# A two-layer hybrid encoder in one launch: softmax ahead in the engines' order, later transposes, another spread of the convolution's taps

## The chip, the cores and the metric

The kernel runs on one core of a Trainium2 chip. The metric is the device time of one launch in microseconds (us). The kernel before takes 1797.9 us, the median of three runs (1797.21 to 1798.3).

Five engines of the core matter. TensorE (PE in the profile) multiplies matrices, VectorE (DVE) and ScalarE (ACT) work on elements and rows, GpSimd (POOL) does little here, and SyncE (SP) starts most DMAs. Each engine takes its own instructions strictly in order. Between engines there are semaphores.

## The reference

The input is a sequence of 512 rows of 1024 numbers, in float32. Two layers follow each other, and each of them computes:

```python
h = rmsnorm(x, norm_mix[i]);  proj = h @ w_in[i]
qa, ka, va, glu_in, qc, kc, vc, gates = split(proj)
ya = diff_attention(qa, ka, va, ...)          # 4 heads, two softmaxes each: a0 - lam * a1
yb = silu(layernorm(depthwise_conv31(a * sigmoid(g))))     # glu_in = a, g; 512 channels, 31 taps
yc = neighbourhood_attention(qc, kc, vc, rpb) # 8 heads, 8x16 window on an 8x64 grid
ga, gb, gc = split(sigmoid(gates))
x = x + (ga*(ya@w_br_a) + gb*(yb@w_br_b) + gc*(yc@w_br_c)) @ w_o[i]
x = x + (silu(rmsnorm(x)@w_ffn_gate) * (rmsnorm(x)@w_ffn_up)) @ w_ffn_down
x = x + sigmoid(rmsnorm(x)@w_ple_gate) * (p[i]@w_ple_in)
```

Here `lam = exp(sum(lq1*lk1)) - exp(sum(lq2*lk2)) + lam_init`, one number per layer, and a last RMSNorm ends the program.

## The kernel before

**Data and products.** Activations are kept transposed, as tiles of 128 channels by 512 rows. Every float32 operand is split into a high part and a low rest, both of type fp32r: ACT rounds the high part (`wh`, line 143) and DVE subtracts it (`wl`, line 157). One product is then three matmuls (`mm3`, lines 177 to 179). Weights come in blocks of up to 128x1024 through rings of three buffers named `wr` (raw), `wh` and `wl`. All blocks go through the same rings, the 256-wide ones of the embedding too (`pin_wh`). So the block three places later writes the buffer of the block that PE has read.

**Order of PE.** PE's order is fixed by the order of the code. A long projection calls `tick()` after every four chunks, that is after 12 matmuls. At each tick the pieces of attention whose time has come put their own matmuls in between. A piece is a generator, and `yield n` hands back until n ticks later.

**Order of the other engines.** A scheduler sets it beforehand, by priorities: mostly the order of the code. Weights get 400 places of lead. Nothing is reordered while the program runs, so an instruction whose input is late holds all behind it on its engine.

**The background taps.** The 124 tap operations of a layer's convolution (`conv_z`, line 160 and a first one at line 525, all on DVE) have slack. The function `background` ties so many of them behind a given instruction. The table `BG` says how many, by stage. They must all be done before the sums of the convolution's layer norm (`conv_ss`, then its split `conv_qk`, then PE's `conv_tr` at line 556).

**The neighbourhood units** (tiles `natten_...`, 16 a layer, `natten_unit`). Each unit issues two blocks of scores (`natten_sc`). DVE adds the bias and takes the minimum (`natten_b`, line 684), ACT exponentiates (`natten_e`), DVE inverts the sums (line 696) and ACT scales. After `yield 2` PE transposes the weights into `natten_tr` (five transposes, lines 708 to 712). ACT and DVE split these into `natten_pt` and the edge tile `natten_a`. After another `yield 2` PE multiplies by the values (`natten_av`, lines 730 and 731). The results go into `natten_y` through DVE.

**The differential units** (tiles `diff_...`). They have scores (`diff_sc`, line 798), a maximum on DVE (`diff_s`, line 895), two exponentials on ACT (`diff_a`, `diff_e`), a combination on DVE (`diff_a`, line 160), eight transposes (`diff_tr`, line 852) and products with the values (`diff_av`). The root-mean-square of a head goes through `diff_tr` as well (line 213, reduced on DVE at line 215 into `diff_sm`). The `diff_tr` tiles share a ring of two banks. The rotary embedding of the queries and keys is a row of DVE operations on `diff_rp`.

**The values** (`values()`, lines 591 to 593 in the profile) accumulate four blocks of the sequence in PSUM, the first three in three banks, the fourth in the bank of `natten_av`.

**Order of the stages in a layer:** gated linear unit, neighbourhood queries and keys and values, gates in between, differential queries and keys and values, `branchc`, `mergea`, one block of `gateb`, the convolution's norm, `mergeb`, output product, feed-forward, embedding.

Of the kernel before, what the change touches and what calls it, by code (L numbers as in the profile page):

```python
# [61 lines left out]
class Net:  # L62
# [246 lines left out]
    def opening(self):  # L309
# [22 lines left out]
        for k in range(KD):  # L332
# [7 lines left out]
            self.split(his[k], los[k], raws[k])  # L340
# [48 lines left out]
    def lambdas(self):  # L389
# [4 lines left out]
        self.tt(pr, lv[:, 0, :].rearrange("p (a b) -> p a b", b=64),  # L394
                lv[:, 1, :].rearrange("p (a b) -> p a b", b=64), ALU.mult)
# [6 lines left out]
        for i in range(L):  # L402
            v = self.nlam[:, i:i + 1]
            nc.vector.tensor_scalar(v, v, lam_init(i), -1.0, ALU.add, ALU.mult)
            nc.vector.tensor_scalar(self.subg[:, i:i + 1], self.par(i, "sub"),
                                    1.0 - lam_init(i), None, ALU.mult)

    def layer(self, i, h, xsrc, xs):
# [4 lines left out]
        if i == 0:  # L413
            self.lambdas()
# [5 lines left out]
        self.drain(self.renorm)  # L420
        self.h = self.hs
# [4 lines left out]
        self.gates(acc, gb, "cc")  # L426
        self.natten_in(3, sn, yc)
        self.gates(acc, gb, "c")
        self.diff_in(0, sd, ya)
        self.gates(acc, gb, "c")  # L430
# [3 lines left out]
        self.gates(acc, gb, "bb")  # L434
        self.diff_in(3, sd, ya)
        self.gates(acc, gb, "ccbbcc")
# [93 lines left out]
    def background(self, after, n):  # L530

        ph, self.phase = self.phase, "conv"
        for _ in range(n):
            i = next(self.todo, None)
            if i is not None:
                self.tc.add_manual_dep(
                    i.ins, after.ins.name,
                    mybir.DependencyInfo(mybir.DependencyClass.NoSync, mybir.DependencyReason.DATA),
                    reason="background")
        self.phase = ph  # L540

# [37 lines left out]
    def values(self, ap, parts):  # L579
# [33 lines left out]
    def natten_in(self, pr, st, ys):  # L613
# [5 lines left out]
        for s, off in enumerate((OFF_QC, OFF_KC)):  # L619
# [3 lines left out]
            if pr == 0:  # L623
# [5 lines left out]
            self.background(self.stt(low, ps, f, nat.bitcast(F32), ALU.mult, ALU.subtract),  # L629
                            self.bg["natten"] if pr or self.i else 0)  # L630
# [37 lines left out]
    def natten_unit(self, pr, half, u, st4, k2, st, box, y):  # L668
# [10 lines left out]
        for t in range(2):  # L679
# [4 lines left out]
            nc.vector.tensor_tensor_reduce(  # L684
                out=b[:, t], in0=sc, in1=b[:, t], scale=-1.0, scalar=3.0e38,
                op0=ALU.add, op1=ALU.min, accum_out=m[:, t:t + 1])
            wide = half != t
            e = two[:, t, 0:NW + 64 * wide]
            own = slice(64 * (qt == 1), 64 * (qt == 1) + NW)
            if wide:  # L690
                pad = slice(0, 64) if qt == 1 else slice(NW, NW + 64)
                nc.gpsimd.memset(e[:, pad], 0.0)
            self.act(e[:, own], b[:, t], AF.Exp, table="exp", scale=-1.0, bias=m[:, t:t + 1],
                     accum_out=m[:, 2 + t:3 + t])
# [44 lines left out]
    def gates(self, acc, gb, names):  # L739
        for n in names:  # L740
            if n == "c":
                self.gate_c(acc, next(self.ms[0]))
            else:
                self.gate_b(gb, next(self.ms[1]), AF.Copy, None)

    def gate_c(self, acc, m):
# [781 lines left out]
```

## Time and profile before

| What | Value |
|---|---|
| median of three runs | 1797.9 us |
| profiled execution, its own time | 1798.02 us |
| its span | 1796.2 us |
| time outside the span | 1.8 us |
| PE busy | 1773.8 us (99%) |
| DVE busy | 1372.2 us (76%) |
| ACT busy | 897.9 us (50%) |

The span is the time from the first to the last recorded instruction of the profiled execution. A busy share is a mean over stages. In the list of waits a row gives the waiting engine, its operation and line, the instruction that it waited for, and then the total, the number and the longest of these waits. A timeline row gives start, duration, engine, line, operation, output and inputs, and in brackets the idle time ahead of it. When several instructions are put into one row the duration is that of all of them. The window view gives, for a stretch of time, each engine's busy time and number of instructions, and then the clock that PE was granted (1.00 is full).

### The profile page before, as it was taken

The numbers are of one execution on the slowest core, as the hardware profiler recorded it, in microseconds if no ns is written. First come the engines' busy times: TensorE is split into PE (matmuls) and PEld (weight loads), VectorE is DVE, ScalarE is ACT, GpSimd is POOL, SyncE is SP. The second block draws the span as 40 slices with busy tenths as digits, with TensorE's granted clock in tenths as the row PEclk, the third lists the DMA queues.
The fourth block names the chain that finished last, engine by engine and source line by source line (L and its number), as shares of the span: only waits on it lengthen the run. The fifth ranks groups of instructions, "written<-read, shape, count | busy, mean of one in ns | idle before, by whom it ended". The sixth has DMA issues, their size and how long they took to land.

```text
span 1796.2 us, 26565 instructions
## 1 busy us (share of the span) xinstructions
PE 1773.8 (99%) x10020; PEld 1553.7 (86%) x10020; DVE 1372.2 (76%) x2112; ACT 897.9 (50%) x1481; POOL 63.5 (4%) x102
## 2 busy tenths in 40 slices
PE   9999999999999999999999999999999999999998
PEld 7887788888899899898878878888888998998987
DVE  7678789898887567587786777988878775775776
ACT  5556554525565245255545564563255552542544
POOL 0000000000000000000000000000000100000000
PEclk9999999999999999999999999999999999999999
DMA  5666444224656456253437664533354662663432
GB/s 186 186 183 171 126 126 106 88 88 159 211 145 182 145 146 191 91 138 121 158 113 194 174 159 127 137 85 99 107 186 152 184 195 73 188 180 110 119 109 95
DMA packets 98385, 257.51 MB, mean 143 GB/s; under 512 B 12881, under 2 KB 17617, under 8 KB 98257
## 3 DMA queue, kind: packets, MB, share of 16 engines
q1 hardware_dynamic: 90912, 231.00, 42.3%
q0 software_dynamic: 6336, 23.07, 7.1%
q8 instruction: 79, 1.29, 0.3%
q10 hardware_dynamic: 1008, 1.75, 0.3%
q14 instruction: 50, 0.40, 0.1%
HBM read 216.44 MB, written 7.86 MB: 125 GB/s over the span
## 4 chain that ended last, share of the span: by engine, by line
PE 93%; DVE 4%; ACT 1%; issue 1%; DMA 0%; POOL 0%; POOLq 0%; DVEq 0%; ACTq 0%
PE ffn_sc L1090 14%; PE ffn_av L1090 7%; PE ffn_mm L178 4%; PE ffn_mm L177 4%; PE ffn_mm L179 4%; PE ffn_tr L1090 4%; PE mergea_mm L177 2%; PE mergea_mm L178 2%; PE mergea_mm L179 2%; PE gatec_mm L178 2%; PE gatec_mm L179 2%; PE gatec_mm L177 2%; PE wo_mm L177 2%; PE wo_mm L178 2%; PE wo_mm L179 2%; PE diff_sc L798 2%
## 5 line engine op out<-in xcount | busy, mean ns | idle before, releaser
L143 ACT ACTIVATE ffn_wh<-ffn_wr 128x1024 fp32r<-128x1024 f32 (+1 forms) x114 | 117.3, 1029 | 183.2 <-PE ffn_mm L178 106.5
L160 DVE SCALAR_TENSOR_TENSOR conv_z<-glu_z,pre_par,conv_z 128x512 f32<-128x512 f32 x240 | 179.3, 747 | 2.9
L157 DVE TENSOR_TENSOR ffn_wl<-ffn_wr,ffn_wh 128x1024 fp32r<-128x1024 f32 (+1 forms) x114 | 134.9, 1184 | 42.5 <-ACT ffn_wh L143 42.0
L1090 PE MATMUL ffn_sc<-wo_h,ffn_wh 128*128 128x256 f32 x704 | 130.4, 283 | 0.0
L1090 PEld LDWEIGHTS ffn_sc<-wo_h,ffn_wh 128*128 128x128 f32 x704 | 110.4, 192 | 0.8
L1090 PE MATMUL ffn_sc<-wo_h,ffn_wl 128*128 128x256 f32 x352 | 99.6, 283 | 0.0
L177 PE MATMUL ffn_mm<-ffn_z,ffn_wh 128*128 128x512 f32 x240 | 93.5, 389 | 0.0
L178 PE MATMUL ffn_mm<-ffn_z,ffn_wh 128*128 128x512 f32 x240 | 93.4, 389 | 0.0
L179 PE MATMUL ffn_mm<-ffn_z,ffn_wl 128*128 128x512 f32 x240 | 93.4, 389 | 0.0
L157 DVE TENSOR_TENSOR ffn_t<-ffn_mm,wo_r 128x512 f32<-128x512 f32 x48 | 33.0, 688 | 76.2 <-PE ffn_mm L179 76.1
L157 DVE TENSOR_TENSOR ffn_wl<-ffn_rp,ffn_wh 128x1024 fp32r<-128x1024 f32 x44 | 53.7, 1221 | 30.0 <-ACT ffn_wh L143 30.0
L143 ACT ACTIVATE mergea_wh<-mergea_wr 128x1024 fp32r<-128x1024 f32 (+1 forms) x32 | 27.1, 847 | 88.8 <-PE mergea_mm L178 80.4
L1090 PEld LDWEIGHTS ffn_sc<-wo_h,ffn_wl 128*128 128x128 f32 x352 | 67.5, 192 | 0.0
L1090 PE MATMUL ffn_sc<-wo_qk,ffn_wh 128*128 128x256 f32 x352 | 67.2, 283 | 0.0
L1090 PE MATMUL ffn_sc<-wo_v,ffn_wh 128*128 128x256 f32 x352 | 67.1, 283 | 0.0
L1090 PE MATMUL ffn_av<-wo_h,ffn_wh 128*128 128x256 f32 x352 | 65.3, 283 | 0.0
L143 ACT ACTIVATE ffn_wh<-ffn_rp 128x1024 fp32r<-128x1024 f32 x44 | 46.4, 1055 | 29.3 <-PE ffn_mm L178 17.5
L143 ACT ACTIVATE natten_e<-natten_b,natten_s 128x256 f32<-128x256 f32 x64 | 32.2, 503 | 47.0 <-issue 42.8
L1090 PEld LDWEIGHTS ffn_sc<-wo_qk,ffn_wh 128*128 128x128 f32 x352 | 54.9, 192 | 0.0
L1090 PEld LDWEIGHTS ffn_av<-wo_h,ffn_wh 128*128 128x128 f32 x352 | 54.9, 192 | 0.0
L1090 PEld LDWEIGHTS ffn_sc<-wo_v,ffn_wh 128*128 128x128 f32 x352 | 54.9, 192 | 0.0
L179 PEld LDWEIGHTS ffn_mm<-ffn_z,ffn_wl 128*128 128x128 f32 x240 | 45.1, 188 | 9.4
(725 smaller groups left out, 5654.4 us busy)
## 6 DMA issues: line engine op xcount, KB each, us to landing
ffn_wr<-w_gu SPq DMA_DIRECT2D x66, 512.0 KB, 4.3
ffn_e<-w_gu SPq DMA_DIRECT2D x32, 512.0 KB, 3.7
ffn_e<-w_gu POOLq DMA_DIRECT2D x32, 512.0 KB, 7.8
ffn_wr<-w_fd SPq DMA_DIRECT2D x32, 512.0 KB, 4.5
natten_wr<-w_in SPq DMA_DIRECT2D x16, 512.0 KB, 4.4
natten_b<-bias SPq DMA_DIRECT2D x32, 256.0 KB, 3.4
gatec_wr<-w_in SPq DMA_DIRECT2D x16, 512.0 KB, 4.6
diff_wr<-w_in SPq DMA_DIRECT2D x16, 512.0 KB, 4.4
```

The lines of the kernel that those rows point to most:

```text
L143: i = self.nc.scalar.activation(out, in_, func, **kw)
L157: return self.nc.vector.tensor_tensor(out, a, b, op)
L160: return self.nc.vector.scalar_tensor_tensor(out, a, s, b, op0, op1)
L177: mm(out, wh, ah, start=first, stop=False)
L178: mm(out, wh, al, start=False, stop=False)
L179: mm(out, wl, ah, start=False, stop=last)
L798: self.nc.tensor.matmul(out, st4[:, u, qs], st[:, ks], start=n == 0, stop=n == 1)
L1090: mm(bank[:, u], w[:, u, kp], t, start=begin and n == 0, stop=False, skip_group_check=True)
```

## The change

It has seven parts.

1. The softmax operations on DVE and ACT, of the neighbourhood and the differential units, get 60 places of priority (`URGENT`).
2. A neighbourhood unit's transposes come three ticks after its scores rather than two.
3. The table of taps changes: two rather than one behind each differential operation that has them, numbers of their own for the gates, one more behind every second `branchc`.
4. `values()` goes through the product's chunks in three stretches (0 to 3, 4 and 5, 6 and 7). The fourth accumulator is taken later.
5. The computation of `lam` moves behind the first neighbourhood queries and keys, tied to `low`, an operation there.
6. The warm-up matmuls at the start are 9, not 10, and the first block's high part is rounded on DVE.
7. `behind()` is a helper that ties one instruction behind another.

Line numbers shift: 143 becomes 144, 157 becomes 158, 160 becomes 161, 177 to 179 become 178 to 180, 215 becomes 216, 895 becomes 910, 556 becomes 565.

```diff
-WARM = 10
-BG = dict(glu=2, natten=3, diff=1, gatec=2, branchc=1, gateb=5, mergea=4, mergea2=3)
+WARM = 9
+BG = dict(glu=2, natten=3, diff=2, branchc=1, mergea=4, mergea2=3)
+URGENT = 60
...
+            if k == 0:
+                nc.vector.tensor_copy(his[0], raws[0])
...
-        if i == 0:
-            self.lambdas()
...
         self.drain(self.renorm)
+        if i == 0:
+            self.lambdas()
...
-        self.gates(acc, gb, "cc")
+        self.gates(acc, gb, "cc", 2)
...
-        self.gates(acc, gb, "bb")
+        self.gates(acc, gb, "bb", 3)
...
-        self.gates(acc, gb, "ccbbcc")
+        self.gates(acc, gb, "ccbbcc", 1)
...
-        for t in range(3):
-            products(t, range(2))
-        for t in range(3):
-            products(t, range(2, 4))
+        for ks in (range(2), range(2, 4)):
+            for t in range(3):
+                products(t, ks)
+        for t in range(2):
+            products(t, range(4, 6))
         accs.append(self.ps("av"))
         products(3, range(4))
         vs = []
+        for t in range(2, 4):
+            products(t, range(4, 6))
         for t in range(4):
-            products(t, range(4, KD))
+            products(t, range(6, KD))
...
-            nc.vector.tensor_tensor_reduce(
+            with self.tc.high_priority(offset=URGENT):
+                nc.vector.tensor_tensor_reduce(
...
-        nc.vector.reciprocal(m[:, 4:6], m[:, 2:4])
-        for t, (_, own) in enumerate(es):
-            self.act(own, own, AF.Copy, scale=m[:, 4 + t:5 + t])
-        yield 2
+        with self.tc.high_priority(offset=URGENT):
+            nc.vector.reciprocal(m[:, 4:6], m[:, 2:4])
+            for t, (_, own) in enumerate(es):
+                self.act(own, own, AF.Copy, scale=m[:, 4 + t:5 + t])
+        yield 3
...
-            self.background(self.tt(acc[m], acc[m], ps, ALU.mult), self.bg["branchc"])
+            self.background(self.tt(acc[m], acc[m], ps, ALU.mult), self.bg["branchc"] + m % 2)
...
+            with self.tc.high_priority(offset=URGENT):
+                nc.vector.tensor_reduce(out=m[:, u:u + 1], in_=sc, op=ALU.max, axis=AX.X,
+                                        negate=True)
```

How the instructions stand is shown at three places of layer 0. The number behind a name tells one tile of that name from another.

**Place 1: DVE, between the last two neighbourhood units and the first differential unit.** `natten_tr_1977` and `natten_tr_1978` before, and `natten_tr_2041` and `natten_tr_2042` after, are the transposes of the sixteenth unit. Before:

```order
L157 TENSOR_TENSOR natten_y_1514<-natten_av_1968,natten_y_1514 64x256
L157 TENSOR_TENSOR natten_pt_1985<-natten_tr_1977,natten_pt_1985 128x512
L157 TENSOR_TENSOR natten_y_1514<-natten_y_1514,natten_av_1968 64x256
L157 TENSOR_TENSOR diff_rp_1921<-diff_rp_1921,diff_r_1589 128x512
L160 SCALAR_TENSOR_TENSOR conv_z_830<-glu_z_316,pre_par_67,conv_z_830 128x512
```

And now, from the second of the differential unit's reductions on; ahead of these rows stand, from the same `natten_y` on, `natten_y`, `natten_a_2043`, three operations on `diff_rp`, two taps and the unit's first reduction:

```order
L910 TENSOR_REDUCE diff_s_2066<-diff_sc_2073 128x1
L158 TENSOR_TENSOR diff_rp_1901<-diff_rp_1901,diff_kh_1829 128x512
L158 TENSOR_TENSOR diff_rp_1971<-diff_rp_1971,diff_r_1567 128x512
L917 RECIPROCAL diff_s_2066<-diff_s_2066 128x1
L161 SCALAR_TENSOR_TENSOR conv_z_1909<-glu_z_318,pre_par_67,conv_z_1909 128x512
L161 SCALAR_TENSOR_TENSOR diff_s_2066<-diff_s_2066,natten_nlam_540,diff_sm_1753 128x1
L161 SCALAR_TENSOR_TENSOR conv_z_1909<-glu_z_318,pre_par_67,conv_z_1909 128x512
L161 SCALAR_TENSOR_TENSOR diff_a_2071<-diff_e_2077,diff_s_2066,diff_a_2071 128x512
L158 TENSOR_TENSOR diff_rp_1971<-diff_rp_1971,diff_r_1569 128x512
L158 TENSOR_TENSOR natten_y_1491<-natten_y_1491,natten_av_2032 64x256
L158 TENSOR_TENSOR diff_rp_1971<-diff_rp_1971 128x512
L158 TENSOR_TENSOR natten_pt_2049<-natten_tr_2041,natten_pt_2049 128x512
```

`natten_pt` of the last unit moved from right behind the first `natten_y` to behind the whole softmax of the first differential unit. On PE the transposes of that unit are now followed by 12 matmuls of `values()`, the four score matmuls, 12 more of `values()`, and then `natten_av`, which reads `natten_pt_2049`.

**Place 2: DVE, in the differential units, from the second score reduction of one unit (the head's fourth) on to the reduction of `diff_tr` at line 215, or 216 now.** Before, the rows are 11:

```order
L895 TENSOR_REDUCE diff_s_2361<-diff_sc_2368 128x1
L157 TENSOR_TENSOR diff_rp_2298<-diff_rp_2298 128x512
L900 RECIPROCAL diff_s_2361<-diff_s_2361 128x1
L160 SCALAR_TENSOR_TENSOR diff_s_2361<-diff_s_2361,glu_nlam_435,diff_sm_2010 128x1
L160 SCALAR_TENSOR_TENSOR diff_a_2366<-diff_e_2372,diff_s_2361,diff_a_2366 128x512
L157 TENSOR_TENSOR diff_rp_2298<-diff_rp_2298,diff_kh_2237 128x512
L157 TENSOR_TENSOR diff_rp_2377<-diff_rp_2377,diff_r_1589 128x512
L525 TENSOR_SCALAR conv_z_2384<-glu_z_319,pre_par_67 128x512
L157 TENSOR_TENSOR diff_wl_2643<-diff_wr_2641,diff_wh_2642 128x1024
L157 TENSOR_TENSOR diff_rp_2377<-diff_rp_2377,diff_r_1591 128x512
L215 TENSOR_REDUCE diff_sm_2453<-diff_tr_2448 128x4
```

Now they are 19, of which these are the last 12:

```order
L161 SCALAR_TENSOR_TENSOR diff_a_2371<-diff_e_2377,diff_s_2366,diff_a_2371 128x512
L158 TENSOR_TENSOR diff_rp_2302<-diff_rp_2302 128x512
L158 TENSOR_TENSOR diff_rp_2302<-diff_rp_2302,diff_kh_2241 128x512
L158 TENSOR_TENSOR diff_rp_2382<-diff_rp_2382,diff_r_1567 128x512
L158 TENSOR_TENSOR diff_wl_2645<-diff_wr_2643,diff_wh_2644 128x1024
L161 SCALAR_TENSOR_TENSOR conv_z_1909<-glu_z_318,pre_par_67,conv_z_1909 128x512
L158 TENSOR_TENSOR diff_rp_2382<-diff_rp_2382,diff_r_1569 128x512
L161 SCALAR_TENSOR_TENSOR conv_z_1909<-glu_z_318,pre_par_67,conv_z_1909 128x512
L910 TENSOR_REDUCE diff_s_2464<-diff_sc_2465 128x1
L158 TENSOR_TENSOR diff_rp_2382<-diff_rp_2382 128x512
L910 TENSOR_REDUCE diff_s_2464<-diff_sc_2471 128x1
L216 TENSOR_REDUCE diff_sm_2458<-diff_tr_2453 128x4
```

From the first reduction of the unit, two rows ahead of these 19 and five ahead of the 11, to the reduction of `diff_tr`, there are now four taps rather than two, seven operations on `diff_rp` rather than six, and the next unit's two score reductions besides.

**Place 3: ACT and DVE at the convolution's norm.** `gateb_mm_3928` (before) and `gateb_mm_3927` (after) are the products that PE computes right ahead of `conv_tr`. ACT before:

```order
L143 ACTIVATE pin_e_3925<-pin_t_3923 128x512
L143 ACTIVATE conv_qk_3915<-conv_ss_3911 128x512
L143 ACTIVATE gateb_wh_4013<-gateb_wr_4012 128x1024
L143 ACTIVATE gateb_v_3977<-gateb_mm_3928 128x512
```

and now:

```order
L144 ACTIVATE pin_e_3924<-pin_t_3922 128x512
L144 ACTIVATE gateb_wh_4012<-gateb_wr_4011 128x1024
L144 ACTIVATE gateb_v_3976<-gateb_mm_3927 128x512
L144 ACTIVATE conv_qk_3914<-conv_ss_3910 128x512
```

DVE before:

```order
L157 TENSOR_TENSOR pin_e_3920<-pin_t_3918,pin_e_3920 128x512
L157 TENSOR_TENSOR gatec_x_3107<-gatec_x_3107,mergea_t_3883 128x512
L160 SCALAR_TENSOR_TENSOR conv_z_3642<-glu_z_924,pre_par_67,conv_z_3642 128x512
L157 TENSOR_TENSOR pin_e_3925<-pin_t_3923,pin_e_3925 128x512
L157 TENSOR_TENSOR conv_ss_3911<-conv_ss_3911,conv_z_3642 128x512
L157 TENSOR_TENSOR conv_qk_3915<-conv_ss_3911,conv_qk_3915 128x512
L157 TENSOR_TENSOR gateb_wl_4014<-gateb_wr_4012,gateb_wh_4013 128x1024
```

and now:

```order
L158 TENSOR_TENSOR gatec_x_3100<-gatec_x_3100,mergea_t_3878 128x512
L161 SCALAR_TENSOR_TENSOR conv_z_3662<-glu_z_902,pre_par_67,conv_z_3662 128x512
L158 TENSOR_TENSOR pin_e_3924<-pin_t_3922,pin_e_3924 128x512
L161 SCALAR_TENSOR_TENSOR conv_z_3662<-glu_z_902,pre_par_67,conv_z_3662 128x512 x3
L158 TENSOR_TENSOR gateb_wl_4013<-gateb_wr_4011,gateb_wh_4012 128x1024
L161 SCALAR_TENSOR_TENSOR conv_z_3662<-glu_z_902,pre_par_67,conv_z_3662 128x512
L158 TENSOR_TENSOR conv_ss_3910<-conv_ss_3910,conv_z_3662 128x512
L158 TENSOR_TENSOR conv_qk_3914<-conv_ss_3910,conv_qk_3914 128x512
```

Four more taps stand ahead of the last `conv_ss`, and the next weight block's split (`gateb_wh`, `gateb_wl`) moved from behind `conv_qk` to ahead of `conv_ss` and `conv_qk`. That block is the third in the ring behind the one that PE reads for the `gateb` product (two 256-wide `pin` blocks lie between), so it takes the same buffer.

More of the change, by code (lines that the diff above doesn't have):

```diff
@@ L535, in background, with behind @@
             if i is not None:
[L536 to L539, printed above, removed]
+                self.behind(i, after)
         self.phase = ph
+    def behind(self, i, after):
+        self.tc.add_manual_dep(
+            i.ins, after.ins.name,
+            mybir.DependencyInfo(mybir.DependencyClass.NoSync, mybir.DependencyReason.DATA),
+            reason="background")
     def conv(self, cs, ys):
@@ L737, in natten_unit, with gates, gate_c @@
         self.tt(y[rs, 1, qs], y[rs, 1, qs].bitcast(F32), av[ro], ALU.add)
[L739 to L742, printed above, removed]
-            else:
-                self.gate_b(gb, next(self.ms[1]), AF.Copy, None)
-    def gate_c(self, acc, m):
+    def gates(self, acc, gb, names, n):
+        for name in names:
+            if name == "c":
+                self.gate_c(acc, next(self.ms[0]), n)
+            else:
+                self.gate_b(gb, next(self.ms[1]), AF.Copy, None, n)
+    def gate_c(self, acc, m, n):
         self.phase = "gatec"
@@ L769, in merge_a, with gate_b @@
             self.background(self.tt(acc[m], acc[m], g, ALU.add), self.bg["mergea2"])
-    def gate_b(self, gs, m, func, table):
+    def gate_b(self, gs, m, func, table, n=5):
         self.phase = "gateb"
@@ L778, in gate_b @@
                 gs += self.parts_of("rp" if m == 2 else "v", [512], 2)
-        self.background(self.act(gs[m], ps, func, table=table), self.bg["gateb"])
+        self.background(self.act(gs[m], ps, func, table=table), n)
     def merge_b(self, ys, acc, gs):
```

58 lines of the change are left out of this document (30 added, 28 removed).

## The prediction

> **What bounds the kernel now.** First the page of the whole execution: busy shares, then the chain that ended last.
>
> ```profile
> PE 1773.8 (99%) x10020; PEld 1553.7 (86%) x10020; DVE 1372.2 (76%) x2112; ACT 897.9 (50%) x1481; POOL 63.5 (4%) x102
> PE 93%; DVE 4%; ACT 1%; issue 1%; DMA 0%; POOL 0%; POOLq 0%; DVEq 0%; ACTq 0%
> ```
>
> PE bounds it: 1796.2 − 1773.8 = 22.4 us of the span are left without PE. The change removes one warm-up matmul and no other work of PE. So the time can only move by PE's waits, and by the clock at which PE runs. Next, therefore, PE's waits:
>
> ```profile
> PE natten_tr L710 <- ACT natten_e L143: 5.1, 2, 2.5
> PE diff_sc L798 <- ACT diff_a L143: 2.3, 2, 1.2
> PE natten_mm L591 <- DVE natten_t L160: 1.7, 1, 1.7
> PE natten_tr L708 <- ACT natten_e L143: 1.6, 2, 0.8
> PE diff_av L591 <- DVE natten_y L157: 1.5, 2, 0.7
> PE diff_av L177 <- DVE diff_v L157: 0.9, 2, 0.5
> PE conv_tr L556 <- DVE conv_qk L157: 0.2, 1, 0.2
> PE conv_tr L556 <- ACT conv_qk L143: 0.2, 1, 0.2
> ```
>
> Those that come twice come once per layer. Then the windows around the longest of them (PE, PEld, DVE, ACT and POOL busy, then the clock):
>
> ```profile
> 174.31:177.72 3.41, 1.61 (x11) 1.36 (x12) 3.20 (x7) 2.77 (x8) 0.15 (x1) 1.00 0.77 193
> 177.73:181.14 3.41, 3.41 (x10) 2.63 (x9) 3.32 (x10) 1.63 (x5) 0.00 (x0) 0.50 0.33 123
> 54.84:58.25 3.41, 2.43 (x11) 2.02 (x12) 2.96 (x5) 1.32 (x2) 0.00 (x0) 1.00 0.94 231
> 1065.19:1068.60 3.41, 3.41 (x13) 2.94 (x14) 3.17 (x5) 1.17 (x3) 0.15 (x1) 0.50 0.72 223
> 352.00:413.50 61.50, 61.50 (x273) 50.96 (x272) 60.18 (x87) 16.44 (x24) 0.00 (x0) 1.00 0.34 104
> ```
>
> After each wait of 2.5 us stands a window of 3.41 us in which PE never stops but has a clock of 0.50. Half of that, **1.7 us**, is lost besides. The wait of 1.7 us at 54 us has no such window behind it. The last row says that DVE is busy 60.18 of 61.50 us ahead of the convolution's norm: there is no room there for work that comes late.
>
> **The waits that go.** Neighbourhood transposes come 12 matmuls later, and the softmax has priority. From the rows of waits, per layer: natten_tr 5.1/2 + 1.6/2 = 3.35, the half-clock window 1.7, diff_sc 2.3/2 = 1.15, diff_av 1.5/2 + 0.9/2 = 1.2. That is 7.4, and **14.8 us** for two layers. The bounds are nothing and this: a row cannot give more than it holds.
>
> At 52 us the wait for natten_t is 1.7. The work on lam that moves away was some small operations on DVE ahead of that chain and a table load on ACT (first row; the second is what PE waits for):
>
> ```profile
> 48.10 1.28 ACT L143 ACT_TABLE_LOAD   x1
> 52.02 0.68 DVE L160 SCALAR_TENSOR_TENSOR natten_t<-natten_t,natten_kh 128x512 fp32r<-128x512 f32 x1
> 5.88 0.80 PE L347 MATMUL pre_mm<-glu_v,pre_y 128*128 128x512 f32 x1 [0.19 <-ACT pre_y L143]
> ```
>
> I take 1.2 of the 1.7, between nothing and all. The third row is the first real matmul, which waited for ACT's rounding; DVE may have that sooner, for 0.3, between nothing and 0.6 (its rounding stood behind one other ACT operation). The gain is 14.8 + 1.5 = **16.3 us**.
>
> **The wait that comes at the last neighbourhood unit.** natten_pt of that unit now stands on DVE behind the first differential unit's softmax. Prices of the rows, from the timeline before at that place:
>
> ```profile
> 193.11 0.29 PE L708 MATMUL natten_tr<-pre_ident,natten_e 128*128 128x128 f32 x1
> 193.24 0.60 PE L710 MATMUL natten_tr<-pre_ident,natten_e 128*128 128x128 f32 x4
> 195.12 0.67 DVE L157 TENSOR_TENSOR natten_pt<-natten_tr,natten_pt 128x512 fp32r<-128x512 f32 x1
> 199.13 0.64 PE L730 MATMUL natten_av<-natten_pt,natten_v 128*128 128x256 f32 x4
> 199.96 0.40 PE L798 MATMUL diff_sc<-diff_x,diff_qk 128*128 128x512 f32 x1
> 202.36 0.75 DVE L160 SCALAR_TENSOR_TENSOR conv_z<-glu_z,pre_par,conv_z 128x512 f32<-128x512 f32 x1
> 203.74 0.42 DVE L157 TENSOR_TENSOR natten_y<-natten_y,natten_av 64x256 fp32r<-64x256 f32 x1
> 204.19 0.69 DVE L157 TENSOR_TENSOR diff_rp<-diff_rp 128x512 f32<-128x512 f32 x1
> 204.80 0.68 DVE L895 TENSOR_REDUCE diff_s<-diff_sc 128x1 f32<-128x512 f32 x1
> 206.38 0.16 DVE L900 RECIPROCAL diff_s<-diff_s 128x1 f32<-128x1 f32 x1
> 206.58 0.22 DVE L160 SCALAR_TENSOR_TENSOR diff_s<-diff_s,glu_nlam,diff_sm 128x1 f32<-128x1 f32 x1
> 206.84 0.75 DVE L160 SCALAR_TENSOR_TENSOR diff_a<-diff_e,diff_s,diff_a 128x512 f32<-128x512 f32 x1
> ```
>
> From start to start, an operation of 128x512 takes 0.61 (204.19 to 204.80), a tap 0.66 and diff_a 0.67 (about 0.08 less than its bar), natten_y 0.45 (203.74 to 204.19), the reciprocal 0.2, the small product 0.26. natten_pt took 0.67. Count from the end of the natten_av ahead of the last transposes. PE needs 0.5 for them, 24 matmuls at 0.227 (24 matmuls lie in the 5.4 us between 193.7 and 199.13), 5.45, and four score matmuls at the same price, 0.9: it wants natten_pt at **6.9**. DVE starts natten_y some 0.25 later and does natten_y 0.45, natten_a, which is half as wide, 0.3, three diff_rp 1.8 and two taps 1.2: 4.0. The scores are there by 3.9 (0.5 + 12 × 0.227 + 0.5 + 0.2). Then two reductions 1.2, four diff_rp 2.4, the reciprocal 0.2, two taps 1.3, small product 0.26, diff_a 0.67, natten_y 0.45, natten_pt 0.67: 4.0 + 7.2 = **11.2**. The wait is 11.2 − 6.9 = 4.3. It is longer than 2.5, so the half clock follows: 1.7. Two layers: **12.0 us**. Bounds per layer: 3 to 8, since the first eight rows may run while PE still multiplies, or DVE may arrive late by the 1.2 that natten_pt needed at 195.12 after its transposes.
>
> **The wait that comes in the differential units.** More taps and the next unit's reductions stand ahead of the diff_sm reduction, which frees one of the two diff_tr banks.
>
> ```profile
> 237.12 0.69 DVE L895 TENSOR_REDUCE diff_s<-diff_sc 128x1 f32<-128x512 f32 x1 [1.51 <-PE diff_sc L798]
> 247.08 0.68 DVE L215 TENSOR_REDUCE diff_sm<-diff_tr 128x4 f32<-128x512 f32 x1
> 248.39 1.04 PE L852 MATMUL diff_tr<-pre_ident,diff_a 128*128 128x128 f32 x8
> 252.03 0.60 PE L226 MATMUL diff_tr<-pre_ident,diff_rc 128*128 128x128 f32 x4
> ```
>
> At 237.12 DVE had waited for PE, so both orders start level there. To the end of diff_sm (247.7) the new order adds two taps, two reductions and one diff_rp, 3.1, less 0.5 that DVE stood idle for ACT: 250.3. PE needs the bank for the second four of its eight transposes, 248.8: a wait of 1.5. Then the transposes of 252.03 need the other bank, which DVE's split of the first four (diff_pt) frees: ahead of its end stand three taps, one diff_rp, diff_a, three small operations and diff_pt itself, 4.4 us. That ends at 254.7, against 252.03 + 1.5 when PE is there: another 1.2. Together 2.7 per layer, **5.4 us**, with no half clock, as behind the 1.7 at 54 us. Bounds per layer: nothing (DVE ahead by 3) and 2.7 + 1.7.
>
> **The wait that comes at the convolution of layer 0.**
>
> ```profile
> 409.04 0.42 ACT L143 ACTIVATE pin_wh<-pin_wr 128x256 fp32r<-128x256 f32 x1 [1.81 <-PE mergea_mm L178]
> 410.42 0.68 DVE L157 TENSOR_TENSOR mergea_t<-mergea_t,mergea_mm 128x512 f32<-128x512 f32 x1
> 413.49 0.68 DVE L157 TENSOR_TENSOR conv_ss<-conv_ss,conv_z 128x512 f32<-128x512 f32 x1
> 414.74 1.04 ACT L143 ACTIVATE gateb_wh<-gateb_wr 128x1024 fp32r<-128x1024 f32 x1
> 414.89 0.50 PE L556 MATMUL conv_tr<-conv_qk,pre_onesr 128*128 128x512 f32 x1 [0.22 <-ACT conv_qk L143]
> 415.81 1.23 DVE L157 TENSOR_TENSOR gateb_wl<-gateb_wr,gateb_wh 128x1024 fp32r<-128x1024 f32 x1 [0.25 <-ACT gateb_wh L143]
> ```
>
> The first row shows the ring: a block's rounding waits for PE's matmuls on an older block. gateb_wh takes the buffer that PE reads until C, the end of the gateb product (414.67 here). Now conv_qk is queued behind it on ACT, and conv_ss behind its rest gateb_wl on DVE. From C: rounding 1.15, rest 1.15, a tap 0.66, conv_ss 0.68, conv_qk 0.63: conv_tr starts at C + 4.3, with its second half 0.2 later, against 0.44 of waits before. That is 4.1, and 1.7 for the clock: **5.8 us**. Bounds: nothing if that buffer is free sooner, and 8 if DVE reaches the block late. In layer 1 I cost this at nothing: no row of conv_tr L556 waits there.
>
> **The sum.** 1798.0 (this execution's own time; 1.8 outside its span) − 16.3 + 12.0 + 5.4 + 5.8 = 1804.9, so **1805 us**. The execution stands 0.1 above the median of 1797.9.
>
> On the clock the Trainium skill has a rule ("TensorE: Matmul & The Clock Gate", Part 1, "The HAM clock gate"): the gate goes to half after at least one idle window of about 3.4 us. By it waits of 2.5 us cost no clock, though the rows at 177.73 and 1065.19 show half clock behind them. What would follow from it is weighed as the last rival.
>
> **Rivals.** (1) *DVE catches up in PE's new pause* (faster). While PE waits 4.3 us for natten_pt, DVE works on; if it keeps a lead of 3 us, diff_sm is on time and the last taps are too, and only the first new wait stays: 1798.0 − 16.3 + 12.0 = 1793.7. Against it: the idle 1.51 at 237.12 says that DVE is already level with PE there, and gateb_wh hangs on PE itself. If natten_pt's wait fell away as well, it would be 1781.7. (2) *The waits come without the half clock*: three windows of 1.7 less, 1799.8, no change. Against it speak the two windows at 0.50. (3) *Lateness is carried on* (slower): in 352 to 413.5 DVE has 1.3 us of room, so diff waits grow to their bound and draw the clock (2 × 1.7), and DVE reaches the block at the convolution 2 to 4 late: 1805 + 3.4 + 4 = 1812. (4) *Waits of 2.5 us cost no clock, those over 3.4 do*: then the 3.4 us of old half clock aren't regained, 1808.3. Against it are the same two rows.
>
> **How the numbers follow.** Forecast 0.42; rival (1) 0.15 and its full form 0.07; (2) 0.14; (3) 0.17; (4) 0.05. A measurement can tell 0.2%, 3.6 us. Slower: 0.42 less 0.02, 0.17, 0.05: 0.62. Faster: 0.07 and most of (1), 0.11: 0.18. Same: 0.20. The range goes from (1) to (3) with its bounds: 1793 to 1816; outside are the full gain and the far ends. The forecast's own range is 1800 to 1811.
>
> **What would show it.** Right: no natten_tr wait of 2.5; a wait of natten_av on natten_pt of 4 us in each layer, near 200 and 1090, with a window at 0.50 behind it; diff_tr waiting on diff_sm near 250; conv_tr at L565 waiting 4 us near 415, with gateb_wl ahead of conv_ss. Wrong: natten_av without a wait, or a new wait in a place that isn't named here, above all in layer 1's convolution.

## The result, and the profile after

The changed kernel takes **1812.8 us** (median of four runs, 1811.5 to 1813.9) against 1797.6 us (1797.2 to 1798.3) before. The ratio is 1.0086, with a 95% interval of 1.0073 to 1.0099: slower by 15 us. The forecast was slower, to 1805 us, within 1793 to 1816. The way, the three places and the range were right. The size was not: +7 was forecast and +15 came, more than twice as much.

The profiled execution took 1813.94 us, 15.9 more than that of before. The first rows are the page's busy times and PE's waits of the changed kernel:

```profile
PE 1780.3 (98%) x10019; PEld 1558.8 (86%) x10019; DVE 1371.0 (76%) x2113; ACT 901.3 (50%) x1480; POOL 64.6 (4%) x102
...
PE diff_tr L866 <- DVE diff_sm L216: 8.5, 4, 2.1
PE natten_av L744 <- DVE natten_y L158: 7.1, 4, 3.3
PE conv_tr L565 <- ACT conv_qk L144: 4.4, 1, 4.4
PE natten_av L744 <- DVE natten_pt L158: 2.0, 4, 0.7
...
PE natten_mm L600 <- DVE natten_t L161: 0.8, 1, 0.8
```

The span is 1812.1 us. PE is idle for 1812.1 − 1780.3 = 31.8 us of it, against 22.4 before: **9.4 us more**. PE is also busy for 1780.3 − 1773.8 = **6.5 us more**, although it has one matmul less: it worked at half clock more often. The two make up the 15.9 us.

The old waits of natten_tr, diff_sc and diff_av (11.4 us together) are gone. Of natten_mm's 1.7 us there are 0.8 left. In their place stand the three waits that the prediction named. The timeline of the changed kernel at the last neighbourhood unit, at the differential units and at the convolution (start, duration, engine, line, operation; in brackets the idle time ahead):

```profile
198.03 0.68 DVE L158 TENSOR_TENSOR diff_rp<-diff_rp,diff_r 128x512 f32<-128x512 f32 x1
198.74 0.42 DVE L158 TENSOR_TENSOR natten_y<-natten_y,natten_av 64x256 fp32r<-64x256 f32 x1
199.31 0.55 PE L744 MATMUL natten_av<-natten_pt,natten_v 128*128 128x256 f32 x1 [3.05 <-DVE natten_y L158]
199.80 0.69 DVE L158 TENSOR_TENSOR natten_pt<-natten_tr,natten_pt 128x512 fp32r<-128x512 f32 x1
200.54 0.80 PE L744 MATMUL natten_av<-natten_pt,natten_v 128*128 128x256 f32 x2 [0.68 <-DVE natten_pt L158]
...
249.23 0.68 DVE L216 TENSOR_REDUCE diff_sm<-diff_tr 128x4 f32<-128x512 f32 x1
250.06 0.83 PE L866 MATMUL diff_tr<-pre_ident,diff_a 128*128 128x128 f32 x4 [2.13 <-DVE diff_sm L216]
254.88 0.60 PE L227 MATMUL diff_tr<-pre_ident,diff_rc 128*128 128x128 f32 x4
...
417.94 1.06 ACT L144 ACTIVATE gateb_wh<-gateb_wr 128x1024 fp32r<-128x1024 f32 x1 [3.98 <-PE gateb_mm L179]
419.22 1.22 DVE L158 TENSOR_TENSOR gateb_wl<-gateb_wr,gateb_wh 128x1024 fp32r<-128x1024 f32 x1
421.86 0.63 ACT L144 ACTIVATE conv_qk<-conv_ss 128x512 fp32r<-128x512 f32 x1 [2.38 <-DVE conv_ss L158]
422.54 1.52 PE L565 MATMUL conv_tr<-conv_qk,pre_onesr 128*128 128x512 f32 x2 [4.41 <-ACT conv_qk L144]
```

At the first place PE stands at 196.26 and waits twice, first for natten_y and then for natten_pt, which stand behind the differential unit's softmax on DVE. At the third place ACT waits 3.98 us for PE to release the ring's buffer, and conv_qk is queued behind that: PE waits for a chain that begins with PE's own matmul.

Now the clock. The windows of the changed kernel around these waits (PE, PEld, DVE, ACT, POOL busy, then the granted clock) end at the clock's own steps, which are 3.41 us apart:

```profile
195.74:199.15 3.41, 0.52 (x3) 0.09 (x1) 3.38 (x9) 0.00 (x0) 0.00 (x0) 1.00 0.55 129
199.15:202.56 3.41, 2.57 (x8) 2.11 (x9) 2.40 (x5) 1.01 (x2) 0.00 (x0) 0.50 0.26 60
202.56:205.98 3.42, 3.42 (x10) 2.65 (x9) 0.42 (x1) 0.00 (x0) 0.00 (x0) 0.50 0.75 172
205.98:209.39 3.41, 3.41 (x17) 2.78 (x16) 1.38 (x3) 1.57 (x5) 0.00 (x0) 1.00 0.34 80
246.94:250.35 3.41, 1.28 (x10) 0.94 (x9) 3.41 (x6) 2.33 (x6) 0.00 (x0) 1.00 0.42 148
250.35:253.76 3.41, 3.41 (x12) 2.74 (x10) 3.41 (x9) 0.72 (x3) 1.46 (x1) 0.50 0.73 171
281.07:284.48 3.41, 1.84 (x11) 1.31 (x9) 3.41 (x7) 1.47 (x4) 0.00 (x0) 1.00 0.43 121
284.48:287.89 3.41, 2.85 (x15) 2.47 (x16) 3.27 (x8) 1.58 (x4) 1.01 (x1) 1.00 0.53 124
421.02:424.43 3.41, 1.89 (x4) 1.26 (x5) 1.79 (x4) 0.63 (x1) 0.00 (x0) 0.50 0.14 43
424.43:427.84 3.41, 3.41 (x10) 2.65 (x9) 3.41 (x7) 2.96 (x6) 0.00 (x0) 0.50 0.01 2
```

And four rows of PE's timeline, two from the second half-clock window and two from behind it:

```profile
204.13 0.63 PE L600 MATMUL diff_mm<-diff_wh,glu_h 128*128 128x512 f32 x1
204.55 0.63 PE L601 MATMUL diff_mm<-diff_wl,glu_h 128*128 128x512 f32 x1
...
206.14 0.40 PE L602 MATMUL diff_mm<-diff_wh,glu_h 128*128 128x512 f32 x1
206.37 0.40 PE L812 MATMUL diff_sc<-diff_qk 128*128 128x512 f32 x1
```

Three things are to be seen. The long waits are followed by two windows at half clock, not one, since the wait's tail leaves the first of them partly idle (2.57 of 3.41). The wait of 2.13 us at 247.9 falls into one window and calls up a half-clock window; the same wait at 282.9 is divided between two windows and calls up none. And the price: from start to start a 128x512 matmul takes 0.43 us in a half-clock window (204.13 to 204.55) and 0.23 at full clock (206.14 to 206.37). So 8 start in a window of 3.41 us rather than 15; the rows count 10 and 17, with those that reach over an edge. A half-clock window in which PE is never idle costs 7 × 0.227 = **1.6 us**, close to the prediction's 1.7. Several expectations below reckon with 1.1, from the 10 of the rows set against 15, and that is too little.

The changed kernel has eight such windows up to its last matmuls (two at 199, one at 250, two at 421, two at 1100, one at 1151), the kernel before has two. PE is busy for 24.2 us in the eight and for 6.8 in the two. With a share of 1.6/3.41 = 0.47 lost, that is 8.1 us more. At the start of the program the changed kernel gets 1.0 of it back: PE's busy time up to its 21st real matmul is 8.86 us rather than 9.84, since it has one warm-up matmul less and the matmuls are 0.43 apart until about 4.6 us rather than 6.9. That leaves 7.1 against the measured 6.5; the rest is not explained.

### The profile page after: what moved, and what is told of

It is laid out like the page before. It is cut to its first block, busy times and chain, and to the rows that moved or that the text cites. A ratio compares the mean times of both kernels' runs of the same rounds, so it can differ in the third digit from the quotient of the medians.

```text
span 1812.1 us, 26533 instructions
## 1 busy us (share of the span) xinstructions
PE 1780.3 (98%) x10019; PEld 1558.8 (86%) x10019; DVE 1371.0 (76%) x2113; ACT 901.3 (50%) x1480; POOL 64.6 (4%) x102
## 4 chain that ended last, share of the span: by engine, by line
PE 91%; DVE 7%; issue 1%; DMA 0%; ACT 0%; POOL 0%; DVEq 0%; SPq 0%; POOLq 0%; ACTq 0%
PE ffn_sc L1107 14%; PE ffn_av L1107 7%; PE ffn_mm L179 4%; PE ffn_mm L178 4%; PE ffn_mm L180 4%; PE ffn_tr L1107 3%; PE mergea_mm L180 2%; PE mergea_mm L178 2%; PE mergea_mm L179 2%; DVE conv_z L161 2%; PE wo_mm L179 2%; PE wo_mm L178 2%; PE wo_mm L180 2%; PE natten_mm L178 1%; DVE diff_rp L158 1%; PE natten_mm L179 1%
## 5 line engine op out<-in xcount | busy, mean ns | idle before, releaser
L910 DVE TENSOR_REDUCE diff_s<-diff_sc 128x1 f32<-128x512 f32 x64 | 42.5, 685 | 26.2 <-PE diff_sc L812 26.2
```

Of the source, the lines that this page charges most:

```text
L910: nc.vector.tensor_reduce(out=m[:, u:u + 1], in_=sc, op=ALU.max, axis=AX.X, negate=True)
```

## The experiments

In all of them the times stand against runs of the kernel before on the same chip, 1797.0 to 1797.8 us in the median.

**Undoing the priority and the table of taps, one by one and together.** First the table, with the old numbers at gates and branchc too (the first of its edits):

```diff
-BG = dict(glu=2, natten=3, diff=2, branchc=1, mergea=4, mergea2=3)
+BG = dict(glu=2, natten=3, diff=1, branchc=1, mergea=4, mergea2=3)
```

> The changed kernel with the table of taps as before (one behind a differential operation, the old numbers for the gates and branchc). At the convolution of layer 0 the block gateb is then split behind conv_qk again, and natten_pt of the last unit stands two rows ahead of the first differential reduction. Theory: conv_tr's wait of 4.4 goes with 2.6 of half clock, and the waits at natten_av shorten to under 1.5 and call up no half clock, which gives another 2 x 5; the waits at diff_tr shrink by two taps, 1.3, so that they call up no half clock either (2 x 1.7 and 4 x 1.3): 1812.8 - 7 - 10 - 8.6 = 1787, 1784 to 1796. Rival, the order at these places comes from the priority of the softmax and the taps matter at the convolution alone: 1812.8 - 7 = 1806.

Measured: **1785.7 us**, ratio 0.9939 (0.9922 to 0.9955). It is faster than the kernel before. PE's waits of this kernel:

```profile
PE diff_tr L866 <- DVE diff_sm L216: 3.7, 4, 1.4
PE diff_tr L227 <- DVE diff_pt L158: 1.8, 2, 1.0
```

No wait of natten_av, none of conv_tr above 0.2, no half clock up to the last matmuls. The sum of the theory holds to 1.3 us, partly by luck: natten_av's wait went whole rather than to 1.5, and a wait on diff_pt came that it did not have. The table of taps alone is worth 27 us in the changed kernel. Then the priority:

```diff
-URGENT = 60
+URGENT = 0
```

> The changed kernel with the softmax's priority set to nothing, all else as changed. The convolution's order stays as changed, natten_pt of the last unit stands seven rows ahead of the first differential reduction, and one reduction fewer stands ahead of diff_sm. Theory: the priority makes the wait at natten_av; without it that falls to under 1.5 with no half clock, -2 x 5, diff_tr's waits get shorter by 0.6 to 1.5 each and lose their half clock, -2 x 1.7 - 4, the convolution keeps its 7, and some of the old wait of diff_sc (2.3) comes back: 1812.8 - 10 - 7.4 + 2.3 = 1798, 1793 to 1802. Rival, the later transposes alone put natten_pt behind too much work: above 1808.

Measured: **1798.3 us**, ratio 1.0007 (0.9998 to 1.0017), no change against before. PE's waits:

```profile
PE diff_tr L866 <- DVE diff_sm L216: 5.0, 4, 1.3
PE conv_tr L565 <- ACT conv_qk L144: 4.4, 1, 4.4
PE natten_av L744 <- DVE natten_y L158: 2.6, 2, 1.4
```

As expected, the convolution's wait stays to the hundredth, since it comes from the taps, and the others shrink below what calls up half clock. And both together:

> The changed kernel with both undone, the priority and the table of taps; the later transposes, the three stretches in values(), the moved lambda and the shorter warm-up remain. It completes the square of priority and taps (both 1812.8, priority alone 1785.7, taps alone 1798.3). Theory: the gain of the old waits comes from the later transposes, and the priority only adds the waits of diff_sc (2.3) and diff_av (2.4): with natten_tr's 6.7 and its half clock (2.3) and natten_mm's 0.9 gone, 1797.6 - 9.9 = 1787.7, some natten_av waits of up to 1 each coming back: 1786 to 1791. Rival, the priority is what removes natten_tr's waits: 1794 or more.

Measured: **1782.8 us**, ratio 0.9921 (0.9906 to 0.9936), 5 us under what was expected. The one wait of more than 1 us that is left in the layers is an old one:

```profile
PE diff_sc L812 <- ACT diff_a L144: 2.3, 2, 1.2
```

This wait is what the priority takes away; for it the kernel with the priority waits 5.5 us at diff_tr (3.7 and 1.8). So the square is: neither 1782.8, priority alone 1785.7 (+2.9), taps alone 1798.3 (+15.5), both 1812.8 (+30.0). The two cost 12 us more together than singly (30.0 − 2.9 − 15.5 = 11.6). What remains of the change without them is worth 15 us of gain.

**Which taps.** The table has two halves, the second tap behind a differential operation, and the other numbers at gates and branchc. One half at a time was put back, first the one at the differential units, with gates and branchc as changed:

```diff
-BG = dict(glu=2, natten=3, diff=2, branchc=1, mergea=4, mergea2=3)
+BG = dict(glu=2, natten=3, diff=1, branchc=1, mergea=4, mergea2=3)
```

> The changed kernel with one tap behind each differential operation as before, and the new numbers for the gates and branchc kept. On DVE natten_pt of the last unit then stands two rows ahead of the first differential reduction; at the convolution the split of gateb stays ahead of conv_ss. Theory: the second tap in the differential units is what makes natten_av and diff_tr wait, and the gates' numbers are what leaves too many taps to the convolution. So conv_tr's wait of 4.4 stays, with its two half-clock windows (1.1 us lost in each, by the count of matmuls in them), and the rest is as with the whole old table (1785.7): 1785.7 + 4.0 + 2.2 = 1791.9, 1790 to 1794. Rival, the number of taps left at the convolution and the second tap only matter together: near 1786 or near 1812.

Measured: 1803.0 us, ratio 1.0030 (1.0019 to 1.0042), 11 us above what was expected. natten_av waits no more, as expected, but the convolution is far worse:

```profile
PE conv_tr L565 <- ACT conv_qk L144: 13.4, 2, 10.7
```

I had overlooked that taps not done in the differential units are left over for the convolution: there PE now waits 10.7 us in layer 0 and 2.7 in layer 1. The gates' new numbers are fewer, so the second tap was needed to keep the total. The other half, with five taps behind each gate b and one behind every branchc as before (one of its edits):

```diff
-        self.gates(acc, gb, "ccbbcc", 1)
+        self.gates(acc, gb, "ccbbcc", 2)
```

> The changed kernel with the old numbers of taps behind gates and branchc, and two taps behind each differential operation kept. natten_pt and diff_sm stand as in the changed kernel; all taps are done well ahead of the last mergea, and conv_ss stands ahead of gateb's product. Theory: conv_tr does not wait, all else waits as in the changed kernel: 1812.8 - 4.4 - 2.2 = 1806.2, 1804 to 1809. Rival, the earlier taps crowd the gates stage and new waits come there: 1810 or more.

Measured: 1806.1 us, ratio 1.0051 (1.0034 to 1.0068), as expected. conv_tr does not wait, and natten_av (9.2 us in all) and diff_tr (8.6 on diff_sm) do as in the changed kernel. A wait of 0.8 on diff_pt is new:

```profile
PE diff_tr L866 <- DVE diff_sm L216: 8.6, 4, 2.1
PE natten_av L744 <- DVE natten_y L158: 7.1, 4, 3.3
```

So the second tap, together with the priority, makes the wait at the last neighbourhood unit and more than half of that on diff_sm (3.9 of 8.5 us stay with one tap). The gates' numbers make the one at the convolution.

**Putting the late rows ahead.** First at the neighbourhood units, for natten_pt, natten_a and natten_y:

```diff
+        with self.tc.high_priority(offset=URGENT + 20):
             self.split(pp[:, 0], pp[:, 1], pt)
```

> The changed kernel, with the split of the neighbourhood transposes (natten_pt, natten_a) and of the results (natten_y) given 80 places of priority, so that on DVE they stand ahead of the first differential unit's softmax again. Theory: both waits of the last natten_av (3.7 us each) and the two windows at half clock behind each (3 us of lost work each) go, and the rest stays: 1812.8 - 2 x 6.7 = 1799.4, 1797 to 1802. Rival, DVE is short of time in the whole stretch and the lateness shows up at the next place: waits of diff_sc or diff_tr grow by what was won, and the time stays above 1808.

Measured: 1813.4 us, ratio 1.0091 (1.0076 to 1.0106): nothing won. The waits of natten_av are gone, and another has their size:

```profile
PE diff_mm L600 <- ACT diff_rp L144: 9.9, 2, 5.0
```

and, in its timeline,

```profile
182.39 0.69 DVE L158 TENSOR_TENSOR diff_rp<-diff_rp,diff_kh 128x512 fp32r<-128x512 f32 x1
188.36 0.60 ACT L144 ACTIVATE natten_pt<-natten_tr 128x512 fp32r<-128x512 f32 x1
192.65 0.60 ACT L144 ACTIVATE diff_rp<-diff_mm 128x512 f32<-128x512 f32 x1 [3.69 <-DMA diff_x<-diff_rp]
```

The rival was right that the wait only moves, though it comes at diff_mm and not at diff_sc or diff_tr. With natten_pt ahead, the last rotary operation on the older diff_rp comes 4.8 us later. In the changed kernel it stood at

```profile
177.60 0.67 DVE L158 TENSOR_TENSOR diff_rp<-diff_rp,diff_kh 128x512 fp32r<-128x512 f32 x1
```

Its copies by DMA are later for it, the ring of two diff_rp buffers is full, ACT cannot empty the PSUM bank of diff_mm, and PE waits for that bank. Then the reduction in the differential units, on top of the old table of taps:

```diff
+        with self.tc.high_priority(offset=0 if spread else URGENT + 20):
             nc.vector.tensor_reduce(out=sm, in_=st, op=ALU.add, axis=AX.X)
```

> The changed kernel with the old table of taps, and the reduction that makes diff_sm given 80 places of priority, so that on DVE it stands ahead of the next unit's softmax. With the old table alone PE still waits 5.5 us at diff_tr (3.7 on diff_sm, 1.8 on diff_pt). Theory: these are the row order's doing, and with the reduction ahead they go: 1785.7 - 4.5 = 1781, 1780 to 1783. Rival, DVE is behind in that stretch whatever the order: the wait moves to diff_pt or diff_av and the time stays within 1 us of 1785.7.

Measured: **1780.0 us**, ratio 0.9906 (0.9891 to 0.9921), the fastest of all, against the 1781 that the theory gave. No wait of diff_tr is left. Of more than 0.5 us within the layers there are, beside ple_tr, which all kernels have, only

```profile
PE natten_mm L601 <- DVE natten_t L161: 0.8, 1, 0.8
PE diff_sc L813 <- DMA diff_x<-diff_rp: 0.7, 1, 0.7
```

So one late row put ahead paid and the other only chose which wait PE gets. They are different rows, and the diff_sm row was not tried with two taps. That DVE has more room with one tap is not shown: from 200 to 290 us it is busy for 75.7 us with the old table and for 68.9 in the changed kernel. What counts is which rows stand ahead of the one that PE waits for.

**The edits alone, in the kernel before.**

```diff
-        yield 2
+        yield 3
         pt = self.ps("tr", (P, 2, 256))
```

> The kernel before with one edit of the change: the neighbourhood transposes three ticks behind the scores rather than two. Theory: this alone removes natten_tr's waits (6.7) and their two half-clock windows (1.1 each): 1797.6 - 8.9 = 1788.7, 1787 to 1791. Rival, the waits only move to natten_av, as natten_pt is made 12 matmuls later: 1794 or more.

Measured: 1793.8 us, ratio 0.9977 (0.9968 to 0.9986), 5 us above what was expected.

```profile
PE diff_av L591 <- DVE natten_y L157: 6.1, 2, 3.1
```

natten_tr waits no more, but the last natten_av is later, and natten_y frees its PSUM bank later. The fourth accumulator of `values()` takes that bank. The rival, that the waits only move, was the nearer one.

> The kernel before with one edit of the change: the softmax's priority of 60 places. Theory: the exponentials come sooner, so natten_tr's waits of 2.5 shrink below what calls up half clock and diff_sc's go, but the taps and the reductions behind diff_sm are put back, which makes diff_tr wait: 1797.6 - 5 - 2.3 - 2.2 + 5 = 1793, 1789 to 1798. Rival, the priority costs nothing where there is one tap: 1788 or less.

Measured: 1801.5 us, ratio 1.0025 (1.0015 to 1.0034), slower where I expected 1793: the same wait, only longer.

```profile
PE diff_av L591 <- DVE natten_y L157: 9.0, 2, 4.6
PE diff_tr L854 <- DVE diff_sm L215: 2.9, 4, 0.7
```

What remains when priority, taps and later transposes are all taken out of the changed kernel:

> The changed kernel with priority, table of taps and later transposes undone: what remains are values() in three stretches, the moved lambda, the warm-up of 9 and the first block's rounding on DVE. Theory: these remove the wait natten_mm by 0.9, the wait of diff_av on natten_y (1.5), and shift the rest little; natten_tr's waits stay as before: 1797.6 - 2.4 = 1795, 1793 to 1797. Rival, the three stretches are what the square without priority and old taps (1782.8) owes its gain to: 1790 or less.

Measured: 1795.2 us, ratio 0.9987 (0.9978 to 0.9996), as expected. Here natten_tr's waits are as before, 5.1 and 1.6 us, and diff_av's are gone. So the later transposes need the three stretches of `values()`, which take the bank later: together with the small parts they bring 14.8 us (1782.8), where the one alone brings 4.0 and the other, with the small parts, 2.5. The three stretches and the small parts were not timed apart.

**Filling PE's waits with work that changes nothing**, products of zeros that are added to an open accumulator; one of the places:

```diff
+            self.fill(self.cur, 10)
             for n in range(2):
                 for k in range(2):
                     mm(av, vs[2 * half + n][:, g, cols], pp[:, k, n], start=n == k == 0, stop=False)
```

> The changed kernel, with products of zeros added on PE just ahead of five of its waits: 10 ahead of the last natten_av of each layer, 7 ahead of the second four transposes after the first and the second head's root-mean-square in each layer, 14 ahead of conv_tr in layer 0. They add zero to accumulators that are open anyway, so nothing else changes, and each batch (2.3, 1.6 and 3.2 us at full clock) is shorter than the time that PE waits there until its data comes (3.7, 2.1 and 4.4 us). Theory of the half-busy window: a window of 3.41 us with PE busy for less than about half of it is followed by a window at half clock, and that one by another unless it is busy throughout. Then the five stretches at half clock (27.3 us in all, some 10 us of lost work) go, the waits' ends stay, and the time falls from 1812.8 by 9 to 12 us, to 1801 to 1804. Rival, the clock costs 1.7 us at each of three waits, as my prediction had it: 1812.8 - 5.1 = 1807.7. Rival, the lost time is the data's lateness and PE's clock has no part in it: 1812.8 or more, as the zeros then delay what follows.

Measured: 1809.1 us, ratio 1.0069 (1.0054 to 1.0084), against 1812.8: a gain of 3.7 us where 9 to 12 were expected. The half-clock windows fell from eight to two. The page and the waits:

```profile
PE 1787.8 (99%) x10081; PEld 1564.7 (87%) x10081; DVE 1370.0 (76%) x2113; ACT 900.7 (50%) x1480; POOL 64.5 (4%) x102
...
PE diff_tr L237 <- DVE diff_pt L158: 1.7, 2, 0.8
```

Without its 62 zeros at 0.227 us PE is busy for 1773.7 us, **6.6 less** than in the changed kernel. The six windows that went held 17.4 us of PE's work, 8.1 us at the share of 0.47, and this execution's start, slower by 0.7 up to the 21st real matmul, takes that back; that makes 7.4. The time by itself lies nearer to the rival of three windows (1807.7) than to the theory; the count of windows and PE's busy time decide against that rival.

The gain is less than 6.6 because a new wait takes some of it back. The filled waits hardly changed (22.5 us with their zeros, 22.0 without). But PE at full clock reaches the next bank of diff_tr sooner and waits there for diff_pt, 0.8 us in each layer, a wait that the half clock had covered. Two other traces bear this out: with natten_pt ahead only layer 0 has the half-clock window at this place, and with the old gate taps only layer 1, and each has the wait of 0.81 for diff_pt in the other layer. The profiled execution is 4.9 us shorter, the median 3.7.

The last run takes the filling to one place, where nothing waits for DVE right afterwards:

> The changed kernel without the priority (1798.3, where conv_tr's wait of 4.4 is followed by the only stretch at half clock, 6.8 us), with 14 products of zeros on PE ahead of conv_tr in layer 0, 3.2 us of its wait. Theory of the half-busy window: the stretch at half clock goes, and as nothing waits for DVE right behind conv_tr the time falls by what it cost, two windows of about 1.1 to 1.3: 1798.3 - 2.4 = 1795.9. Rival, work that PE does more slowly there hides DVE's lateness, so nothing is won: 1798.3.

Measured: 1797.6 us, ratio 1.0001 (0.9992 to 1.0010), not to be told from 1798.3 without the filling. In the traces of the kernel without the priority and of this one, the first start of conv_tr's own matmuls and of ple_tr (in the tile view: number, durations, first and last start):

```profile
L565 PE MATMUL conv_tr<-conv_qk,pre_onesr x2: 796/796/796, 415.3 to 416.0; 128*128 128x512 f32 x2
L214 PE MATMUL ple_tr<-pre_ident,ple_ss x4: 272/273/300, 907.8 to 908.2; 128*128 128x128 f32 x4
...
L568 PE MATMUL conv_tr<-conv_qk,pre_onesr x2: 499/502/505, 414.7 to 415.4; 128*128 128x512 f32 x2
L214 PE MATMUL ple_tr<-pre_ident,ple_ss x4: 272/273/300, 905.4 to 905.7; 128*128 128x128 f32 x4
```

From the one to the other it is 492.5 us without and 490.7 with the filling: 1.8 us. The stretch at half clock is two windows long, but its first is mostly over when conv_tr starts: from there PE works 4.3 us at half clock, which at the share of 0.47 costs 2.0. In that profile layer 1 had a half-clock window of its own, behind waits that called up none in the other kernel. So this run shows the price in its trace, not in its median, which the rival forecast better.

## Where the prediction was right, and which step of it failed

- **The bound and the waits that go** were right. natten_tr, diff_sc and diff_av have no wait left. Their windows at half clock were two, as stated, and 1.7 was close to the 1.6 of each. natten_mm gave 0.9 of the 1.2 taken. The gain was not the priority's doing, though: the square shows the later transposes with the three stretches and the small parts as its source, and the priority as a cost of 2.9. The prediction put the two edits into one sentence and one number.
- **The wait at the last neighbourhood unit** was forecast as 4.3 per layer and was 3.05 + 0.68 = 3.7 in layer 0 and 3.26 + 0.74 = 4.0 in layer 1, plus 0.7 in each layer at an earlier unit, which I had not summed: 9.1 in all, against 8.6. That the totals lie so near is in part luck. The row that held it was natten_y first and natten_pt then.
- **The wait in the differential units is one of the two terms that failed**: 5.4 forecast, 8.5 measured. I counted it at the first head alone, with 1.5 for diff_sm. The second head has the same rows and the same 2.13 us (at 282.9). The second wait forecast there, of diff_tr on diff_pt, did not come in the changed kernel; the filled kernel shows that the half clock covered it.
- **The wait at the convolution** was right row by row: 4.4 forecast as 4.3, gateb_wl at 1.1 us behind the end of gateb's product (422.54 − 4.41 = 418.13) where 1.15 was put. In layer 1 there is none, as costed.
- **The clock is the term that failed most.** My sum had 5.1 for three new windows and took 3.4 away for the two old ones, +1.7. PE's busy time rose by 6.5. The size of a window was about right; the steps at fault are "the half clock follows: 1.7", one window behind each long wait, and "with no half clock" in the differential units. A wait of 3.7 to 4.4 us called up two windows, and one of the two waits of 2.13 in each layer called up one, since it fell into one window. So there were eight windows, and three were forecast. By the length of a wait I had tried to say what only PE's busy share in each window says.

The idle time was thus forecast as 5.2 (8.6 + 5.4 + 4.1 − 12.9 of old waits and the start) and was 9.4; the clock as 1.7 and was 6.5. Of the rivals, the one in which DVE catches up is refuted: all three waits came. So is the one without half clock, and the one in which only waits over 3.4 us cost clock: a wait of 2.13 did. The one in which lateness is carried on came to the measured time, 1812, and was half right: the waits in the differential units did grow and draw the clock, but the one at the convolution did not grow.

The prediction drew on the Trainium skill ("TensorE: Matmul & The Clock Gate", Part 1, "The HAM clock gate") for the rule that the gate closes after an idle window of about 3.4 us. The step of 3.41 us agrees with the clock's records here. That the window must be idle does not: one with PE busy for 1.28 of 3.41 us did it.

## What to carry to other kernels

A change of priority is a change of the whole row on an engine: what was put ahead is seen in the code, what was put behind only in the order of each engine, and there the first thing to look for is whatever PE needs next, at every repetition of the place. What it costs depends on the other work in that row: with the changed table of taps a priority that costs 3 us came to cost 14.5. And where two edits come together, time them in a square: here one half of the change was worth 15 us of gain and the other 30 us of loss.

## What the runs showed of the hardware that I had not expected

From the clock's records in the traces of all 14 kernels (before, after and the twelve experiments), with PE's busy share worked out for each window of 3.41 us: all 20 windows at full clock in which PE was busy for at most 0.44 were followed by a window at half clock. Of the 13 windows from 0.45 to 0.57, four were. Of those at 0.58 and more none was. Out of half clock the step is different: after the 13 half-clock windows in which PE was busy for 0.78 or less the clock stayed at half, and after all of those at 0.87 and more it went back to full. So a wait is priced by where it falls. 2.1 us within one window cost up to another 1.6 (0.8 of it would have been a wait for diff_pt), the same 2.1 us across a boundary cost nothing more, and a wait that reaches into the half-clock window keeps the next one slow as well. What decides between 0.45 and 0.57 stays open.

The price shows in plain times too. Of 32 executions of the kernel before on one chip, the 13 with a mean granted clock of 0.999 took 1796.3 us on average and the 6 with 0.997 took 1799.1. One half-clock window takes 3.41 × 0.5 / 1796 = 0.00095 off that mean, so this is 2.8 us for about two windows.
